# Moving the residual adds of a down projection, the end of an attention chunk and the last norm's scaling

## The chip, the cores and the metric

The kernel runs on one core of a Trainium2 chip. The metric is the device time of one execution in microseconds (us). The kernel before takes 2182.29 us, the median of three runs (2181.57 to 2185.2). The engines are named as in the profile: PE (TensorE) with its weight loads PEld, DVE (VectorE), ACT (ScalarE), POOL (GpSimd), and SP (SyncE), whose queue issues all DMAs of this kernel.

## The reference

One decoder layer on x of 2048 positions by 1024 columns, in float32. A norm and one input projection feed two mixers: chunked gated linear attention with 4 heads (GLA), and a short convolution. An output projection and the residual follow, then a SwiGLU feed-forward network with its residual, then a last norm:

```
h = rmsnorm(x, norm1_g);  proj = h @ w_in
o_gla = rmsnorm(gla_chunked(q, k, v, log_a), gla_norm_g) * silu(p_g)
x = x + concat([o_gla, o_conv]) @ w_out
h2 = rmsnorm(x, norm2_g)
x = x + (silu(h2 @ w_ffn_gate) * (h2 @ w_ffn_up)) @ w_ffn_down
return rmsnorm(x, norm_f_g)          # D_MODEL 1024, D_FF 2816
```

## The kernel before, in words

The positions are worked on in two halves of 1024, each as two blocks j of 512 columns; the 1024 features are 8 tiles of 128 rows (d = 0 to 7, `KD`). A tile is 128 partitions by 512 float32, 256 KB. Every float32 matrix product is made of three passes on high and low parts: `split` turns a tile into a rounded high part (ACT, L144) and the remainder (DVE, L145), and `product_step` (L316) issues high·high, high·low and low·high (L321, L322, L323).

The large projections are cut into **units**. A `unit` (L325) computes a 2 by 2 block of result tiles (two row tiles r, two column blocks j) in Strassen's manner: seven products in place of eight, in the order of `PRODUCTS` (L34). Its weights come in one load (`raw`, two buffers); `unit_weights` (L298) makes four sums of weight quarters on POOL (L304, L305, L306, L311) and splits seven quarters into `wq` tiles (four buffers). Its operands ("B11", "T1", ...) were stored as high and low pairs of 512 KB (`op`, pool `opp`, 28 buffers). Results collect in PSUM banks; `copied` (L341, ACT) takes a bank to an SBUF tile, `plus` (L345, DVE) adds a bank to one.

The stages run in this order: input projection of half 0 and half 1 (GLA's work of a half beside it), output projection of both halves, and then for each half `ffn_up` and `ffn_down`. Smaller work is written as generators in the list `background`; `tick` (in `mul`) advances the first of them by one step after every second product. `split_later` and `store_split` write the feed-forward operands through three buffers `so` to the DRAM tensors shown as sa_B and sa_T. `bt` takes a tile from a pool of 11 buffers in this part of the kernel (`fx`).

`gla_half` (L569) is such a generator. For every chunk of 128 positions it makes the scores, yields, loads the next chunk and makes the outputs (`gla_outputs`, L628, which ends with `osb`, L662), yields, and finishes the chunk (`gla_finish`, L665: four transposes of `osb` into the bank `ot`, L669; the product with gain and gate, L670; a split; stores), and yields.

`ffn_down` (L836) runs over four groups u of hidden row pairs (two, three, three and three), and within each over four units (d0 = 0, 2, 4, 6), 16 units per half. The result tiles y[d, j] gather all groups. In u = 0 the sixteen tiles y are first loaded from the residual s_x1 (shown as sx; L846 to L851), seven pairs in buffers of `opp`. Each unit's four results are then added to y, three by POOL and the one still in PSUM by DVE (L862 to L865). In the last group, half 0 stores y for `finish_later`, which norms it in the background of half 1; half 1 sums squares on the way (`sum_squares`, L691) and ends with `last_unit` (L892), which computes eight half products without the seven-product scheme, makes rstd per block (`norm`, L901, `finish_rstd`, L163), and scales by gain and rstd in `scale` (L907): five tiles per block by DVE in one three-operand operation (L914), three by ACT and POOL (L911, L912).

The order on each engine is set by a scheduler in the build, which models the instructions' times and waits; within SP's queue the DMAs go out one after the other, and one that waits holds those behind it. `tc.issue_after` keeps an instruction behind another in that order.

Of the kernel before, what the change touches and what calls it, by code (L numbers as in the profile page):

```python
# [10 lines left out]
F32 = mybir.dt.float32  # L11
# [36 lines left out]
def tile_hymba_block(ctx, tc, x, xt, win, wa, wgu, wout, wffn, wdown, wdown_first, small, out):  # L48
# [30 lines left out]
    )  # L79
    one_t = ones[:, 0:1]  # L80
    sml = const.tile([P, N_SMALL], F32, name="sml")
    nc.sync.dma_start(sml[:], small)
# [64 lines left out]
    def rsqrt(y, v, l, y0):  # L147

        act.activation(l, v, AF.Ln)
        act.activation(y0, l, AF.Exp, scale=-0.5)  # L150
        dve.tensor_tensor(l, y0, y0, ALU.mult)
        dve.scalar_tensor_tensor(l, l, -0.5, v, ALU.mult, ALU.mult)
        dve.scalar_tensor_tensor(y, l, 1.5, y0, ALU.add, ALU.mult)
# [8 lines left out]

    def finish_rstd(v, tot, n):  # L163
        l, y0 = bt("l"), bt("y0")
        dve.tensor_scalar(v[:], tot[:], 1.0 / n, EPS, ALU.mult, ALU.add)
        rsqrt(v[:], v[:], l[:], y0[:])

# [156 lines left out]

    def unit(src, ops):  # L325


        w = unit_weights(src)

        def mul(i, o=None):  # L330
            first = o is None
            o = bank() if first else o
            n, m = PRODUCTS[i]
            for k in range(len(ops[m])):
                product_step(o, w[n], ops[m], k, first)
            tick()
            return o

        def copied(name, o):
            t = tt(name)  # L340
            act.activation(t[:], o[:], AF.Copy)  # L341
            return t

        def plus(t, o):
            dve.tensor_tensor(t[:], o[:], t[:], ALU.add)  # L345
            return t


        oa = mul(0)
        c11 = copied("c11", oa)  # L350
        ob = mul(1)
        c22 = copied("c22", ob)
        mul(2, oa)
        c12 = copied("c12", oa)
        plus(c11, mul(3))
        mul(4, oa)
        plus(c22, oa)
        mul(5, ob)
        plus(c12, ob)
        mul(6, oa)  # L360
        return [(0, 0, c11, False), (1, 1, c22, False), (0, 1, c12, False), (1, 0, oa, True)]

# [206 lines left out]
    def gla_half(half):  # L569
# [3 lines left out]
        with tc.issue_after(tables.ins):  # L573
            nxt = gla_load(*chunks[0])
        for n, (b, t) in enumerate(chunks):
            cur = nxt
            s = gla_scores(b, t, *cur)
            yield
            if n + 1 < len(chunks):
                nxt = gla_load(*chunks[n + 1])  # L580
            o = gla_outputs(b, t, *s)
            yield
            gla_finish(b, t, *o)
            done.add((b, t))
            yield

# [249 lines left out]
    def ffn_down(half):  # L836

        y = {}
        for u, m0 in enumerate(GROUPS):
# [52 lines left out]
    def last_unit(src, ops, b12, y, ssq):  # L892
# [7 lines left out]

        def norm(j, qs):  # L901
            tot = bank("tot")
            for i, q in enumerate(qs):
                pe.matmul(tot[:], ones[:], q[:], start=i == 0, stop=i == len(qs) - 1)
            finish_rstd(qs[0], tot, D)

        def scale(j, rb):  # L907
            for d in range(KD):
                yy = y[d, j]
                if d % 3 == 1:  # L910
                    act.activation(yy, yy, AF.Copy, scale=col(C_GF + d))  # L911
                    pool.tensor_tensor(yy, yy, rb[:], ALU.mult)  # L912
                else:
                    dve.scalar_tensor_tensor(  # L914
                        yy, yy, col(C_GF + d), rb[:], ALU.mult, ALU.mult
                    )
                load(out[2 + j, :, d, :], yy)

        qs = [ssq[:1], ssq[1:]]
        for j in range(2):  # L920
            for r in range(2):
# [8 lines left out]
                dve.tensor_tensor(yy, o[:], yy, ALU.add)  # L930
                q = tt("q")
                act.activation(q[:], yy, AF.Square)
                qs[j].append(q)
                if j and not r:
                    norm(0, qs[0])
        norm(1, qs[1])
        for j in range(2):
            scale(j, qs[j][0])

# [132 lines left out]
```

## Time and profile before

| what | value |
|---|---|
| median of three runs | 2182.29 us |
| profiled execution | 2184.78 us |
| its span, first to last instruction | 2183.0 us |
| granted PE clock, mean | 0.982 |
| DMA: moved, mean rate | 467.65 MB, 214 GB/s |
| first product of u = 0 on PE, half 0 and half 1 | 1264.49 and 1915.31 us |
| end of VectorE's last operation | 2177.78 us |

All times inside the kernel are from the span's start. A row of the timeline is start, length, engine, line, operation, tiles and count, and in brackets the idle time before it with what ended it. A row of the waits is the engine and line that waited, what ended the wait, the total, the count and the longest. A row of the groups is busy time and mean ns of one, then the idle time of the engine before them and what ended it. In a row of the windows, each engine's busy time has its instruction count behind it, and the last three numbers are the granted clock, the DMA engines' mean busy share and GB/s. A line such as `op<-sa_T` is an operand load, `raw<-in_wdown_first_dram` the weights of a unit of u = 0.

### The profile page before, as it was taken

Reading aid. Unit: us, or ns where it says so; the run is one execution under the profiler, and the core shown is the slowest. Engines: PE = TensorE matmul, PEld = TensorE weight load, DVE = VectorE, ACT = ScalarE, POOL = GpSimd, SP = SyncE. Lnnn points to the kernel's source line nnn. Section 1 sums busy time; section 2 is a strip of 40 time slices with the busy share of each in tenths; the row PEclk is TensorE's granted clock in tenths of the full one; section 3 lists DMA queues with packets and bytes.
Section 4 is the critical chain, followed back from the end, with each engine's and each line's share of the span. In section 5 each row is a group of like instructions: output and inputs, shape, how many; then the busy total and the mean of one; then the engine's idle time right before and its main releaser. Section 6 shows DMA issues by size and latency. Waiting matters only on the chain.

```text
span 2183.0 us, 26899 instructions
## 1 busy us (share of the span) xinstructions
PE 2048.8 (94%) x9137; PEld 1656.3 (76%) x9137; DVE 1460.2 (67%) x2039; ACT 996.5 (46%) x1940; POOL 985.5 (45%) x706
## 2 busy tenths in 40 slices
PE   4899899999998999999999989998999999989996
PEld 3577677877887887788888868887888888867774
DVE  7859975557763496787877566544666656668755
ACT  4555434564544245455555433333444544434442
POOL 4526431112201273555655456664544445357663
PEclk9999999999999999999999999999999999999998
DMA  4259667532586793466454595698353443598772
GB/s 147 71 202 321 215 246 258 150 111 91 156 289 198 295 309 138 164 234 223 174 227 174 214 357 209 245 347 348 116 183 135 159 160 134 221 361 315 304 266 101
DMA packets 189978, 467.65 MB, mean 214 GB/s; under 512 B 19856, under 2 KB 65168, under 8 KB 180112
## 3 DMA queue, kind: packets, MB, share of 16 engines
q1 hardware_dynamic: 189840, 465.93, 59.2%
q8 instruction: 72, 1.18, 0.2%
q14 instruction: 66, 0.54, 0.1%
HBM read 297.03 MB, written 168.82 MB: 213 GB/s over the span
## 4 chain that ended last, share of the span: by engine, by line
PE 68%; DVE 13%; DMA 9%; ACT 4%; issue 3%; POOL 2%; SPq 1%; DVEq 0%; ACTq 0%; POOLq 0%
PE mm L321 20%; PE mm L323 20%; PE mm L322 20%; DVE wq L145 2%; DVE h L431 2%; DMA op<-shT 1%; DVE op L145 1%; PE mm L709 1%; PE mm L710 1%; PE mm L712 1%; DMA op<-sm 1%; DMA op<-sa_T 1%; DVE c L345 1%; DMA raw<-in_wdown_first_dram 1%; DVE so L145 1%
## 5 line engine op out<-in xcount | busy, mean ns | idle before, releaser
L321 PE MATMUL mm<-op,wq 128*128 128x512 f32 x2495 | 984.2, 396 | 50.9 <-ACT c L341 22.2
L322 PE MATMUL mm<-op,wq 128*128 128x512 f32 x2495 | 977.9, 392 | 4.1 <-DVE op L145 4.1
L323 PE MATMUL mm<-op,wq 128*128 128x512 f32 x2495 | 967.2, 393 | 14.9 <-DVE wq L145 14.5
L145 DVE TENSOR_TENSOR wq<-raw,wq 128x512 fp32r<-128x512 f32 (+2 forms) x628 | 526.6, 845 | 337.8 <-ACT wq L144 335.6
L144 ACT ACTIVATE wq<-raw 128x512 fp32r<-128x512 f32 (+2 forms) x628 | 365.1, 587 | 580.2 <-PE mm L323 408.3
L321 PEld LDWEIGHTS mm<-op,wq 128*128 128x128 f32 x2495 | 471.7, 189 | 167.7 <-ACT c L341 30.7
L323 PEld LDWEIGHTS mm<-op,wq 128*128 128x128 f32 x2495 | 471.6, 189 | 124.7 <-DVE wq L145 24.4
L322 PEld LDWEIGHTS mm<-op,wq 128*128 128x128 f32 x2495 | 472.1, 189 | 102.9 <-DVE op L145 5.1
L306 POOL TENSOR_TENSOR raw<-s,raw 128x512 f32<-128x512 f32 (+2 forms) x98 | 131.5, 1342 | 461.5 <-DVE wq L145 427.2
L345 DVE TENSOR_TENSOR c<-mm,c 128x512 f32<-128x512 f32 x294 | 201.6, 686 | 102.6 <-PE mm L323 97.9
L304 POOL TENSOR_TENSOR s<-raw 128x512 f32<-128x512 f32 (+2 forms) x98 | 130.9, 1336 | 210.8 <-DMA raw<-in_wffn_dram 90.5
L341 ACT ACTIVATE c<-mm 128x512 f32<-128x512 f32 x294 | 170.7, 586 | 31.9 <-PE mm L323 30.8
L311 POOL TENSOR_TENSOR raw<-raw 128x512 f32<-128x512 f32 (+2 forms) x98 | 129.0, 1317 | 119.7 <-DVE wq L145 104.2
L865 POOL TENSOR_TENSOR y<-c,y 128x512 f32<-128x512 f32 x90 | 135.9, 1515 | 92.0 <-DVE c L345 91.8
L691 POOL TENSOR_TENSOR ssx<-ssx,q 128x512 f32<-128x512 f32 x52 | 75.9, 1472 | 144.1 <-ACT q L690 143.6
L305 POOL TENSOR_TENSOR raw<-raw 128x512 f32<-128x512 f32 (+2 forms) x98 | 137.2, 1400 | 4.7
L145 DVE TENSOR_TENSOR so<-t,so 128x512 fp32r<-128x512 f32 x100 | 88.0, 889 | 40.2 <-ACT so L144 39.9
L709 PE MATMUL mm<-op,wq 128*128 128x512 f32 x256 | 101.3, 396 | 0.0
L710 PE MATMUL mm<-op,wq 128*128 128x512 f32 x256 | 100.5, 393 | 0.0
L144 ACT ACTIVATE wq<-s 128x512 fp32r<-128x512 f32 (+2 forms) x98 | 57.5, 587 | 92.0 <-PE mm L323 87.6
L144 ACT ACTIVATE so<-t 128x512 fp32r<-128x512 f32 x100 | 62.7, 629 | 66.5 <-DMA sa_B<-so 35.3
L145 DVE TENSOR_TENSOR wq<-s,wq 128x512 fp32r<-128x512 f32 (+2 forms) x98 | 79.3, 810 | 14.8 <-ACT wq L144 14.2
(170 smaller groups left out, 1856.2 us busy)
## 6 DMA issues: line engine op xcount, KB each, us to landing
raw<-in_wffn_dram SPq DMA_DIRECT2D x44, 1024.0 KB, 5.6
sa_T<-so SPq DMA_DIRECT2D x88, 512.0 KB, 5.0
op<-sa_T SPq DMA_DIRECT2D x88, 512.0 KB, 8.4
sa_B<-so SPq DMA_DIRECT2D x69, 512.0 KB, 3.8
op<-sa_B SPq DMA_DIRECT2D x69, 512.0 KB, 8.6
raw<-in_win_dram SPq DMA_DIRECT2D x24, 1024.0 KB, 5.9
raw<-in_wdown_dram SPq DMA_DIRECT2D x24, 768.0 KB, 6.8
y<-sx SPq DMA_DIRECT2D x64, 256.0 KB, 6.7
```

What stands on the lines that cost most here:

```text
L144: last_hi[:] = [act.activation(hi, src, AF.Copy)]
L145: return dve.tensor_tensor(lo, src, hi.bitcast(F32), ALU.subtract)
L304: pool.tensor_tensor(s1, a21, a22, ALU.add)
L305: pool.tensor_tensor(a21, a11, a21, ALU.subtract)
L306: pool.tensor_tensor(a11, s1, a11, ALU.subtract)
L311: pool.tensor_tensor(a12, a12, a11, ALU.subtract)
L321: pe.matmul(o[:], wh, xh, start=first and k == 0, stop=False, skip_group_check=True)
L322: pe.matmul(o[:], wh, xl, start=False, stop=False, skip_group_check=True)
L323: return pe.matmul(o[:], wl, xh, start=False, stop=k == n - 1, skip_group_check=True)
L341: act.activation(t[:], o[:], AF.Copy)
L345: dve.tensor_tensor(t[:], o[:], t[:], ALU.add)
L865: eng.tensor_tensor(yy, c[:], yy, ALU.add)
```

## The change

- **finish_rstd.** ACT's Ln reads the summed squares straight from PSUM, with scale and bias in the same instruction; VectorE still makes the scaled sum for the Newton step, which is now a function of its own and can write into a PSUM bank.
- **unit(into=...).** In u = 0 the unit copies and adds its results directly in the tiles y, which aren't loaded with residuals; the fourth result is also copied by ACT. In u = 1 and u = 2 each unit loads two residual tiles (`x1`, for j = u - 1) and POOL adds them to y after the unit's own adds.
- **gla_half.** A chunk's finish comes after the next chunk's scores; the last one's comes at the end.
- **last_unit.** The gains are applied by ACT ahead of the norm (all sixteen tiles), the squares of r = 0 are added by POOL to the running sum so that the norm sums two tiles instead of three, and rstd stays in PSUM (`rb`), from which VectorE scales six tiles per block; ACT copies it to SBUF for POOL's two tiles.

```diff
+    eps = const.tile([P, 1], F32, name="eps")
+    dve.memset(eps[:], EPS)
...
         act.activation(y0, l, AF.Exp, scale=-0.5)
+        newton(y, v, l, y0)
+
+    def newton(y, v, l, y0):
         dve.tensor_tensor(l, y0, y0, ALU.mult)
...
-    def finish_rstd(v, tot, n):
+    def finish_rstd(v, tot, n, rb=None):
         l, y0 = bt("l"), bt("y0")
+        act.activation(l[:], tot[:], AF.Ln, bias=eps[:], scale=1.0 / n)
+        act.activation(y0[:], l[:], AF.Exp, scale=-0.5)
         dve.tensor_scalar(v[:], tot[:], 1.0 / n, EPS, ALU.mult, ALU.add)
-        rsqrt(v[:], v[:], l[:], y0[:])
+        newton((v if rb is None else rb)[:], v[:], l[:], y0[:])
...
-    def unit(src, ops):
+    def unit(src, ops, into=None):
...
-        def copied(name, o):
-            t = tt(name)
+        def copied(name, o, at):
+            t = tt(name) if into is None else into[at]
...
         mul(6, oa)
+        if into is not None:
+            copied("c21", oa, (1, 0))
...
+        o = None
         for n, (b, t) in enumerate(chunks):
             cur = nxt
             s = gla_scores(b, t, *cur)
             yield
+            if o is not None:
+                gla_finish(*chunks[n - 1], *o)
+                yield
             if n + 1 < len(chunks):
                 nxt = gla_load(*chunks[n + 1])
             o = gla_outputs(b, t, *s)
             yield
-            gla_finish(b, t, *o)
-            done.add((b, t))
-            yield
+        gla_finish(b, t, *o)
+        done.add((b, t))
+        yield
...
-            if u == 0:
-                for d in range(KD):
-                    pair = opp.tile([P, 2, PB], F32, name="y", tag="op") if d < KD - 1 else None
-                    for j in range(2):
-                        y[d, j] = bt("y")[:] if pair is None else pair[:, j, :]
-                        with tc.issue_after(raw_loads[-1].ins):
-                            load(y[d, j], s_x1[2 * half + j][d][:])
...
+                if u == 0:
+                    for d in (d0, d0 + 1):
+                        if d < KD - 1:
+                            pair = opp.tile([P, 2, PB], F32, name="y", tag="op")
+                        for j in range(2):
+                            y[d, j] = pair[:, j, :] if d < KD - 1 else bt("y")[:]
+                    unit(src, ops, {(r, j): y[d0 + r, j] for r in range(2) for j in range(2)})
+                    continue
+                xs = []
+                if u < 3:
+                    for d in (d0, d0 + 1):
+                        xs.append((y[d, u - 1], bt("x1")))
+                        load(xs[-1][1][:], s_x1[2 * half + u - 1][d][:])
...
+                for yy, x1 in xs:
+                    pool.tensor_tensor(yy, x1[:], yy, ALU.add)
...
-        def norm(j, qs):
-            tot = bank("tot")
-            for i, q in enumerate(qs):
-                pe.matmul(tot[:], ones[:], q[:], start=i == 0, stop=i == len(qs) - 1)
-            finish_rstd(qs[0], tot, D)
+        def gain(d, j):
+            act.activation(y[d, j], y[d, j], AF.Copy, scale=col(C_GF + d))
+
+        def norm(j, q):
+
+            tot, rb = bank("tot"), bank("rb")
+            pe.matmul(tot[:], ones[:], ssq[j][:], start=True, stop=False)
+            pe.matmul(tot[:], ones[:], q[:], start=False, stop=True)
+            finish_rstd(ssq[j], tot, D, rb)
+            act.activation(ssq[j][:], rb[:], AF.Copy)
+            return rb
 
         def scale(j, rb):
             for d in range(KD):
-                yy = y[d, j]
-                if d % 3 == 1:
-                    act.activation(yy, yy, AF.Copy, scale=col(C_GF + d))
-                    pool.tensor_tensor(yy, yy, rb[:], ALU.mult)
-                else:
-                    dve.scalar_tensor_tensor(
-                        yy, yy, col(C_GF + d), rb[:], ALU.mult, ALU.mult
-                    )
-                load(out[2 + j, :, d, :], yy)
+                eng, by = (pool, ssq[j]) if d in (2, 5) else (dve, rb)
+                eng.tensor_tensor(y[d, j], y[d, j], by[:], ALU.mult)
+                store(out[2 + j, :, d, :], y[d, j])
+
+        for d in range(KD - 2):
+            for j in range(2):
+                gain(d, j)
...
-                q = tt("q")
-                act.activation(q[:], yy, AF.Square)
-                qs[j].append(q)
+                q[j] = tt("q")
+                act.activation(q[j][:], yy, AF.Square)
+                gain(KD - 2 + r, j)
+                if not r:
+                    pool.tensor_tensor(ssq[j][:], ssq[j][:], q[j][:], ALU.add)
                 if j and not r:
-                    norm(0, qs[0])
-        norm(1, qs[1])
+                    rbs.append(norm(0, q[0]))
+        rbs.append(norm(1, q[1]))
```

More of the change, by code (lines that the diff above doesn't have):

```diff
@@ L349, in unit @@
         oa = mul(0)
-        c11 = copied("c11", oa)
+        c11 = copied("c11", oa, (0, 0))
         ob = mul(1)
-        c22 = copied("c22", ob)
+        c22 = copied("c22", ob, (1, 1))
         mul(2, oa)
-        c12 = copied("c12", oa)
+        c12 = copied("c12", oa, (0, 1))
         plus(c11, mul(3))
@@ L899, in last_unit @@
             act.preload_act_table_set("natural_log_exp_and_others")
-        def norm(j, qs):
-            tot = bank("tot")
-            for i, q in enumerate(qs):
-                pe.matmul(tot[:], ones[:], q[:], start=i == 0, stop=i == len(qs) - 1)
-            finish_rstd(qs[0], tot, D)
+        def gain(d, j):
[7 more added lines that the diff above has]
+            return rb
         def scale(j, rb):
             for d in range(KD):
-                yy = y[d, j]
-                if d % 3 == 1:
-                    act.activation(yy, yy, AF.Copy, scale=col(C_GF + d))
-                    pool.tensor_tensor(yy, yy, rb[:], ALU.mult)
-                else:
-                    dve.scalar_tensor_tensor(
-                        yy, yy, col(C_GF + d), rb[:], ALU.mult, ALU.mult
-                    )
-                load(out[2 + j, :, d, :], yy)
-        qs = [ssq[:1], ssq[1:]]
+                eng, by = (pool, ssq[j]) if d in (2, 5) else (dve, rb)
[4 more added lines that the diff above has]
+                gain(d, j)
+        q, rbs = {}, []
         for j in range(2):
@@ L930, in last_unit @@
                 dve.tensor_tensor(yy, o[:], yy, ALU.add)
-                q = tt("q")
-                act.activation(q[:], yy, AF.Square)
-                qs[j].append(q)
+                q[j] = tt("q")
[3 more added lines that the diff above has]
+                    pool.tensor_tensor(ssq[j][:], ssq[j][:], q[j][:], ALU.add)
                 if j and not r:
-                    norm(0, qs[0])
-        norm(1, qs[1])
+                    rbs.append(norm(0, q[0]))
+        rbs.append(norm(1, q[1]))
         for j in range(2):
-            scale(j, qs[j][0])
+            scale(j, rbs[j])
     act.preload_act_table_set("natural_log_exp_and_others")
```

## The prediction

> **What bounds the kernel now.** I read the page first: the engines' busy times, then the chain that ended last.
>
> ```profile
> span 2183.0 us, 26899 instructions
> PE 2048.8 (94%) x9137; PEld 1656.3 (76%) x9137; DVE 1460.2 (67%) x2039; ACT 996.5 (46%) x1940; POOL 985.5 (45%) x706
> PE 68%; DVE 13%; DMA 9%; ACT 4%; issue 3%; POOL 2%; SPq 1%; DVEq 0%; ACTq 0%; POOLq 0%
> ```
>
> TensorE (PE) is busy for 94% of the span and the chain runs mostly through its matmuls. The change leaves these as they are, but for two norm matmuls less. So a gain can only come out of the span less PE's busy time, 2183.0 - 2048.8 = 134 us, and out of stretches with a slow clock. I therefore looked for the places where PE stops beside the changed code. Next come windows: the first two group units of each half's down projection up to the start of group u1 (half 0, then half 1), two slices inside the first stall, the slice after it, and a stretch without a stall. The columns are the length, the busy time of PE, PEld, DVE, ACT and POOL with their instructions, the granted clock, DMA's share and GB/s.
>
> ```profile
> 1264.49:1316.07 51.58, 42.34 (x176) 33.78 (x174) 34.78 (x51) 20.42 (x46) 32.20 (x30) 0.90 0.89 343
> 1915.31:1970.35 55.04, 44.24 (x178) 34.06 (x177) 40.31 (x53) 23.75 (x52) 34.90 (x31) 0.91 0.94 359
> 1290.00:1295.00 5.00, 0.00 (x0) 0.00 (x0) 0.69 (x1) 1.21 (x2) 0.00 (x0) 0.54 1.03 419
> 1295.00:1300.00 5.00, 3.77 (x9) 3.00 (x10) 3.21 (x5) 2.67 (x8) 3.85 (x5) 0.50 0.81 329
> 2005.00:2037.00 32.00, 32.00 (x140) 25.75 (x138) 22.49 (x26) 16.05 (x34) 30.32 (x24) 1.00 0.77 293
> ```
>
> The last row gives PE's pace: 32.00/140 = 0.229 us a matmul. At that pace the first two rows need 176 x 0.229 = 40.3 and 178 x 0.229 = 40.8 us. They take 51.58 and 55.04, so **11.3 and 14.3 us are lost in group u0**. In the middle of the loss PE does nothing while DMA is full (share 1.03, 419 GB/s), and after it the granted clock is 0.50 for some 5 us. The waits of the two places say who comes last (half 0, then half 1):
>
> ```profile
> ACT so L144 <- DMA sa_B<-so: 10.3, 2, 9.9
> PE mm L321 <- ACT wq L144: 8.5, 1, 8.5
> POOL s L304 <- DMA raw<-in_wdown_first_dram: 7.8, 1, 7.8
> ```
>
> ```profile
> ACT so L144 <- DMA sa_B<-so: 11.3, 2, 10.6
> PE mm L321 <- ACT wq L144: 9.3, 1, 9.3
> POOL s L304 <- DMA raw<-in_wdown_first_dram: 8.7, 1, 8.7
> ```
>
> PE waits for ACT's weight split, ACT is held in its queue by a split for a store buffer (so) whose store hasn't gone out, and unit 2's weights (raw) land late too. Both are DMAs that stand in SyncE's queue behind the residual loads, as SP's timeline shows:
>
> ```profile
> 1261.38 14.04 SPq L136 DMA_DIRECT2D y<-sx  x14
> 1275.81 0.32 SPq L139 DMA_DIRECT2D sa_B<-so  x1
> 1276.48 1.67 SPq L136 DMA_DIRECT2D op<-sa_B  x3
> 1278.52 2.40 SPq L136 DMA_DIRECT2D op<-sa_T  x4
> 1281.70 1.59 SPq L136 DMA_DIRECT2D y<-sx  x2
> 1284.41 1.48 SPq L139 DMA_DIRECT2D sa_B<-so  x2
> 1286.86 1.61 SPq L136 DMA_DIRECT2D raw<-in_wdown_first_dram  x2
> ```
>
> **The change part by part.** The sum is made against the profiled execution: 2184.78 us, 1.78 more than its span and 2.49 above the median of 2182.29; its differences are then taken off the median.
>
> *Group u0.* The sixteen 256 KB loads of y go, and the stores and the third raw load no longer stand behind them. They took SP from 1261.38 to about 1275.4. In the built order the third raw load then has only stores and no op load ahead of it, so I expect it at about 1275 instead of 1286.86, and the so buffers come free as much earlier. Unit 2 then starts without a stop and the clock stays up. The whole loss is the most this can give: 11.3 + 14.3 = 25.6 us.
>
> What is late next? SP is in order, and in the built program the weight load for u1's first unit now stands ahead of all 21 operand loads of u1, of which seven (three and four in the rows above) went out before. That load waits for its buffer, that is for the last split of unit 2. Unit 2 would start at about 1287 and last some ten us, so the buffer comes free at about 1292. DMA's own rate over this stretch is this row, from the DMA view of 1242 to 1297:
>
> ```profile
> DMA packets 7132, 21.78 MB, mean 396 GB/s; under 512 B 796, under 2 KB 796, under 8 KB 7129
> ```
>
> 512 KB (0.524 MB) at 396 GB/s is 1.32 us; 21 of them are 27.8 us, and the weights ahead of them (0.79 MB) 2 us. The last operand lands at about 1292 + 2 + 27.8 = 1322, or 1324 with two us to land. u1 would start 11.3 us earlier, at 1304.8, and its first unit (63 matmuls, 14.4 us) ask for that operand near 1318 to 1319. **New wait: 4 us in half 0**, and 5 in half 1, where two 256 KB x1 loads share the queue with it. At best it is 0, at worst it takes all back. I take u0 at -(11.3 - 4) - (14.3 - 5) = **-16.6 us**, bounds -25.6 and 0. The adds that go (twelve on Pool, four on VectorE per half) were off the path; the four copies that come, 0.6 us each like L149, are hidden by ACT having 20.42 us of work in 51.58, and would cost 2.4 us per half without that cover.
>
> The Trainium skill, "TensorE: Matmul & The Clock Gate", section "HAM oscillation — how this bites in real kernels", holds that an idle gap above about 3.4 us drops TensorE to half rate; the 0.50 row agrees. By that rule a residual wait in one piece would cost up to its own drop again, about 2 us per half, and in pieces nothing. I keep the pieces.
>
> *Groups u1 and u2.* Each of 16 units gets two 256 KB loads and two adds on Pool. The adds that u0 loses stood elsewhere, so here the work is more. Pool's cover is read by group (half 0 u1 and u2, half 1 u1 and u2; four units of 14.3 us each); then come the group of Pool's adds and, for later, a VectorE add with one operand in PSUM:
>
> ```profile
> 1316.00:1373.00 57.00, 57.00 (x254) 47.18 (x253) 33.76 (x46) 20.67 (x41) 37.45 (x30) 1.00 0.60 226
> 1373.00:1430.00 57.00, 57.00 (x252) 46.92 (x251) 28.54 (x44) 20.10 (x40) 35.55 (x29) 1.00 0.64 246
> 1971.00:2028.00 57.00, 56.77 (x248) 45.87 (x248) 47.04 (x57) 25.47 (x51) 45.49 (x34) 1.00 0.85 317
> 2028.00:2085.00 57.00, 52.73 (x226) 41.77 (x225) 41.35 (x52) 21.58 (x40) 38.31 (x29) 1.00 0.75 281
> ```
>
> ```profile
> L865 POOL TENSOR_TENSOR y<-c,y 128x512 f32<-128x512 f32 x90 | 135.9, 1515 | 92.0 <-DVE c L345 91.8
> ```
>
> ```profile
> L734 DVE TENSOR_TENSOR y<-y,mm x32: 669/678/690, 660.4 to 833.8; 128x512 f32<-128x512 f32 x32
> ```
>
> An add takes 1.515 us, eight of them 12.1 us per group. Pool then has 49.6, 47.7, 57.6 and 50.4 us of work in 57. Three groups keep 6 us or more free. In u1 of half 1 Pool is full, 0.6 us over. Queued behind an x1 add are the next unit's weight sums (L304 to L311), for which ACT's splits wait, and then PE. I take **+3 us**: the 0.6 and about 2.4 where sums come late; bounds 0 and 12.1, the whole of u1's adds.
>
> Here a rule speaks against the change. The Trainium skill, "SBUF — State Buffer", section "Who interferes with whom", says that a VectorE instruction with two SBUF inputs and a GpSimd instruction that reads SBUF lock each other out for a whole instruction. By it every added Pool add can hold up one weight split for up to 1.5 us, 12 us on top of VectorE's 47.04 in u1 of half 1. That is 59 of 57, and the sum would be about +2 more. It bears on the rival below.
>
> *Attention chunks.* The transposes of a chunk's output (ot, L669) are what PE waits on:
>
> ```profile
> L669 PE MATMUL ot<-ident,osb 128*128 128x128 f32 x64 | 10.2, 284 | 11.2 <-DVE osb L662 11.2
> ```
>
> ```profile
> 658.86 5.57 DMA y<-in_xt_dram
> 664.56 0.69 DVE y L734
> 665.99 1.08 PE ot L669 x4
> ```
>
> The second fence is cut from the chain at the largest case: VectorE's L662, which makes osb, comes behind an L734 that waits for a DMA, and the transposes behind both. With the chunk's end a step later, 12 to 56 matmuls (2.7 to 12.8 us at 0.229) stand between in the built order; the three waits together are 11.2 us. I take **-10.5 us**: 0.7 stays. If PE merely waits for the next thing of that same late VectorE queue, -0 to -4 is left; so bounds -11.2 and 0.
>
> *The last norm.* Before, VectorE and SP end the program in this order:
>
> ```profile
> 2159.29 0.68 DVE L930 TENSOR_TENSOR y<-mm,y 128x512 f32<-128x512 f32 x1
> 2160.61 6.53 DVE L914 SCALAR_TENSOR_TENSOR y<-y,sml,ssx 128x512 f32<-128x512 f32 x5
> 2167.06 0.68 DVE L165 TENSOR_SCALAR ssx<-tot 128x512 f32<-128x512 f32 x1
> 2171.27 6.51 DVE L914 SCALAR_TENSOR_TENSOR y<-y,sml,ssx 128x512 f32<-128x512 f32 x5
> ```
>
> ```profile
> 2162.51 16.40 SPq L136 DMA_DIRECT2D out_dram<-y  x16
> ```
>
> ```profile
> L912 POOL TENSOR_TENSOR y<-y,ssx 128x512 f32<-128x512 f32 x6 | 9.2, 1562 | 18.3 <-DVE ssx L153 18.3
> L914 DVE SCALAR_TENSOR_TENSOR y<-y,sml,ssx 128x512 f32<-128x512 f32 x10 | 13.0, 1366 | 0.1
> L149 ACT ACTIVATE l<-ssx 128x512 f32<-128x512 f32 x6 | 3.8, 632 | 9.8 <-DVE ssx L165 9.8
> ```
>
> The last scale ends at 2171.27 + 6.51 = 2177.78. After: the six products of j=0 read rstd in PSUM, and a two-operand VectorE op with one operand there took 0.68 (L734) against 1.3 for L914: 6 x 0.68 = 4.1 us, from 2159.9 to 2164.0. In the built order the last L930 stands behind them, to 2164.7. Then come ACT's square 0.63, the second norm's matmuls (estimated at four paces, 0.9), Ln and Exp 2 x 0.63, three VectorE steps 2.1 (0.68 to 0.7 each, as L165) and six products 4.1: 2164.7 + 9.0 = 2173.7. Pool's two products, 0.63 + 2 x 1.56 from 2169.6, end at 2173.3. So -4.1 (the stores behind it as before), and +0.5 for sixteen gains on ACT in u3: **-3.6 us**, bounds -5.5 and +2 (all six at L914's 1.3).
>
> *finish_rstd.* VectorE's step beside Exp instead of ahead of Ln saves 0.68 at most where PE waits for a norm, at the start: **-0.5**, bounds -0.7 and 0.
>
> Sum: -16.6 + 3 - 10.5 - 3.6 - 0.5 = **-28.2 us**; 2184.78 becomes 2156.6, and the median 2182.29 becomes **2154.1**.
>
> **The rivals.** *A, DMA keeps up:* u1's operands come in time because the queue drains during units 2 and 3, and Pool has room. For it: DMA's share is only 0.60 in u1 of half 0. Against it: 419 GB/s at full share while 21 loads are due. u0 -25.6, Pool 0: -40.2, 2142.1. *B, the wait moves on:* PE leaves ot and stands at the next matmul that needs a split from the same blocked VectorE. For it: the L734 ahead waits for DMA either way. Against it: weights are split up to four quarters ahead. -28.2 + 8 = -20.2, 2162.1. *C, Pool half bound:* the sums come late in u1 and u2 of half 1, 12 us instead of 3: -19.2, 2163; with B, 2171. *D, slower:* Pool is the bound in u1 and u2. Its queue is in order, so every x1 add stands ahead of the next unit's weight sums and delays them; SP too stands at an x1 load whose buffer that add must free, with the next weights behind it. 32 adds x 1.515 = 48.5 us instead of 3 gives -28.2 + 45.5 = +17.3, 2199.6. It decides for slower once more than 28.2 + 3 = 31.2 us, 21 of the 32 adds, are on the path. For it: 45.49 of 57. Against it: 6 us or more free in the three other groups. *E:* the change doesn't do what it says; the built order shows the y loads gone from u0 and the chunk ends later, so hardly.
>
> **How the numbers follow.** Forecast (2147 to 2159) 0.47; A 0.15; B or C or both (2159 to 2173) 0.25; D and parts of it 0.09; within 0.2% of before, with E, 0.04. 0.2% (4.4 us) is about what a measurement of this kernel can tell from no change. Faster 0.87, same 0.04, slower 0.09. The range holds the forecast, A with a little more at its low end, and B and C: 2138 to 2173; D lies outside.
>
> **What would show it.** In the changed kernel's profile: the windows at u0 have no slice with PE at 0 and clock 0.5; the third raw load goes out near 1275 less what the chunks gave; new PE waits of a few us at the start of u1 end in op<-sa_T or op<-sa_B DMAs; L669 has under 1 us of idle; the scales stand at 0.69 and the last ends about 4 us nearer to PE's last product. Wrong would be: PE waits for ACT wq with Pool L306 or L311 behind it for over 10 us in u1 and u2 (D), a 9 us stop at u0 still there, or an idle time of some 8 us that turns up at other lines of the attention stretch (B).

## The result and the profile after

The changed kernel takes **2169.37 us** (median of five runs, 2163.8 to 2172.21) against 2182.29 us before (five runs, 2177.67 to 2187.82). The medians differ by 12.9 us. The ratio is 0.9933, with a 95% interval of 0.9916 to 0.9951: 0.67% or some 14.6 us faster (10.7 to 18.3), about half of the 28.2 us that were forecast. The profiled execution took 2172.21 us and is the slowest of the five; keep that in mind where two traces are compared by absolute times. Differences of stages suffer less from it: a second kernel with the same down projection (the second of experiment 1) repeats the rows below within 1.8 us.

The page after, its engines and its chain:

```profile
span 2170.2 us, 26909 instructions
PE 2055.1 (95%) x9133; PEld 1658.8 (76%) x9133; DVE 1447.5 (67%) x2034; ACT 1009.1 (46%) x1960; POOL 993.6 (46%) x714
PE 71%; DVE 11%; DMA 8%; issue 4%; ACT 3%; POOL 3%; SPq 1%; DVEq 0%; POOLq 0%; ACTq 0%
```

The line numbers are now the changed kernel's: a split is L146 (ACT) and L147 (VectorE), a unit's three passes L328 to L330, its weight sums L311 to L318, the adds to y L884 and the added x1 adds L891.

PE's idle time fell from 134 to 115 us, but its modelled busy time rose by 6, since matmuls that trickle in are counted longer (in u1's first unit below, 19.84 us for 74 after against 16.30 before). To find the stages, I cut both traces at the same matmuls. The three passes of the units come in the same order and number in both (2495 each), so the n-th of them in one is the n-th in the other. That gives windows with equal work, with edges within a few matmuls of the groups': u0 of half 0, u1's first unit (72 matmuls, nine of them the next unit's), the same two in half 1, and there the **last stretch**, from that point to the end of u2's first unit. Before:

```profile
1265.80:1316.10 50.30, 41.06 (x170) 32.69 (x170) 33.70 (x49) 20.00 (x45) 31.75 (x29) 0.90 0.89 341
1316.10:1332.40 16.30, 16.30 (x74) 13.49 (x73) 10.31 (x14) 6.25 (x13) 10.94 (x9) 1.00 0.99 398
1913.90:1971.70 57.80, 47.00 (x189) 36.25 (x189) 42.15 (x56) 25.08 (x54) 36.61 (x32) 0.91 0.94 362
1971.70:1988.50 16.80, 16.67 (x73) 13.44 (x73) 15.60 (x19) 7.64 (x15) 11.55 (x9) 1.00 1.03 402
1988.50:2047.20 58.70, 56.97 (x246) 45.43 (x245) 44.43 (x54) 26.74 (x51) 46.32 (x35) 1.00 0.85 322
```

After:

```profile
1252.30:1291.00 38.70, 38.58 (x169) 31.40 (x168) 29.61 (x46) 22.17 (x48) 18.45 (x19) 1.00 0.67 262
1291.00:1315.00 24.00, 19.84 (x74) 13.24 (x73) 7.53 (x12) 5.83 (x12) 8.59 (x8) 0.97 1.03 406
1899.80:1945.70 45.90, 43.74 (x189) 35.02 (x188) 35.04 (x55) 28.29 (x57) 21.42 (x21) 1.00 0.81 317
1945.70:1969.60 23.90, 20.54 (x74) 14.02 (x74) 10.37 (x17) 7.04 (x14) 9.70 (x9) 0.93 1.03 405
1969.60:2036.90 67.30, 59.78 (x245) 46.42 (x244) 46.93 (x53) 26.70 (x51) 54.92 (x41) 0.95 0.91 341
```

Read the rows pairwise, by length. Group u0 went from 50.30 to 38.70 and from 57.80 to 45.90: **23.5 us gained**, with PE idle for 0.1 and 2.2 us instead of 9.2 and 10.8 and the clock at 1.00. Right behind it u1's first unit went from 16.30 to 24.00 and from 16.80 to 23.90: **14.8 us given back**, with DMA full (1.03). In half 1 the last stretch went from 58.70 to 67.30: **8.6 us more given back**, with Pool at 54.92 us instead of 46.32. Of these 8.6 us, 5.8 are idle time of PE (7.5 instead of 1.7) and 2.8 slower matmuls at a clock of 0.95 instead of 1.00. These stages alone sum to 0. The gain that is left lies elsewhere: 12.8 us from the first unit's first product to u0 of half 0, where the attention chunks are, and 4.1 behind the last product (20.3 us instead of 24.4). Against it stand 3.3 us between the rows of the two halves and 1.6 between the last stretch and the last product.

The operand waits are seen in the waits of the changed kernel from 1291 to 1315, the cause in SP's timeline ahead of it:

```profile
ACT wq L146 <- DMA raw<-in_wdown_dram: 11.4, 1, 11.4
...
PEld mm L328 <- DMA op<-sa_B: 2.9, 4, 0.8
```

```profile
1269.90 0.37 SPq L138 DMA_DIRECT2D raw<-in_wdown_first_dram  x1
1279.01 0.33 SPq L138 DMA_DIRECT2D raw<-in_wdown_dram  x1
1279.43 1.64 SPq L138 DMA_DIRECT2D op<-sa_B  x3
1281.16 3.77 SPq L138 DMA_DIRECT2D op<-sa_T  x6
1287.44 2.88 SPq L138 DMA_DIRECT2D op<-sa_B  x3
1291.28 2.88 SPq L138 DMA_DIRECT2D op<-sa_T  x3
1295.12 2.88 SPq L138 DMA_DIRECT2D op<-sa_B  x3
```

SP issues nothing between 1270.3 and 1279.0: it stands at u1's weights, whose buffer isn't free, and all 21 operand loads are behind. The waits for op come in pieces of at most 0.8 us. ACT's wait of 11.4 us is for the next weights, those of u1's second unit: they go out at 1300.25 behind most of the operands, ACT splits them at 1311.12, and PE stops for 1.5 us.

The attention chunks' transposes, L669 before, wait for nothing now:

```profile
L682 PE MATMUL ot<-ident,osb 128*128 128x128 f32 x64 | 9.6, 273 | 0.0
```

The end, four of VectorE's rows from the last unit on:

```profile
2150.68 3.68 DVE L937 TENSOR_TENSOR y<-y,rb 128x512 f32<-128x512 f32 x6 [0.66 <-ACT ssx L931]
2154.27 0.69 DVE L954 TENSOR_TENSOR y<-mm,y 128x512 f32<-128x512 f32 x1
2157.68 0.69 DVE L172 TENSOR_SCALAR ssx<-tot 128x512 f32<-128x512 f32 x1 [2.73 <-ACT l L170]
2161.16 3.68 DVE L937 TENSOR_TENSOR y<-y,rb 128x512 f32<-128x512 f32 x6 [0.66 <-ACT ssx L931]
```

Six scales take 3.68 us instead of 6.5 for five, and the last residual add (L954) stands behind the first six, as the order of the program had it. The last scale ends at 2164.84.

### The profile page after: what moved, and what is told of

Same layout as the page of the kernel before. It is cut to its first block, busy times and chain, and to the rows that moved or that the text cites. A ratio compares the mean times of both kernels' runs of the same rounds, so it can differ in the third digit from the quotient of the medians.

```text
span 2170.2 us, 26909 instructions
## 1 busy us (share of the span) xinstructions
PE 2055.1 (95%) x9133; PEld 1658.8 (76%) x9133; DVE 1447.5 (67%) x2034; ACT 1009.1 (46%) x1960; POOL 993.6 (46%) x714
## 4 chain that ended last, share of the span: by engine, by line
PE 71%; DVE 11%; DMA 8%; issue 4%; ACT 3%; POOL 3%; SPq 1%; DVEq 0%; POOLq 0%; ACTq 0%
PE mm L328 21%; PE mm L330 21%; PE mm L329 20%; DVE wq L147 2%; DVE h L440 2%; DMA op<-sa_T 2%; PE mm L722 2%; PE mm L725 2%; PE mm L723 2%; DMA raw<-in_wdown_dram 1%; DVE op L147 1%; DMA op<-sa_B 1%; DVE so L147 1%; ACT wq L146 1%; DVE c L352 1%
## 5 line engine op out<-in xcount | busy, mean ns | idle before, releaser
L328 PE MATMUL mm<-op,wq 128*128 128x512 f32 x2495 | 987.7, 398 | 38.6 <-ACT c L348 18.2
L330 PE MATMUL mm<-op,wq 128*128 128x512 f32 x2495 | 972.0, 394 | 18.8 <-DVE wq L147 18.0
L147 DVE TENSOR_TENSOR wq<-raw,wq 128x512 fp32r<-128x512 f32 (+2 forms) x628 | 532.1, 854 | 345.0 <-ACT wq L146 338.9
L146 ACT ACTIVATE wq<-raw 128x512 fp32r<-128x512 f32 (+2 forms) x628 | 365.2, 587 | 583.4 <-PE mm L330 408.5
L328 PEld LDWEIGHTS mm<-op,wq 128*128 128x128 f32 x2495 | 473.4, 190 | 159.1 <-ACT c L348 25.4
L330 PEld LDWEIGHTS mm<-op,wq 128*128 128x128 f32 x2495 | 473.4, 190 | 130.4 <-DVE wq L147 30.7
L352 DVE TENSOR_TENSOR c<-mm,c 128x512 f32<-128x512 f32 x270 | 185.2, 686 | 101.2 <-PE mm L330 98.5
L311 POOL TENSOR_TENSOR s<-raw 128x512 f32<-128x512 f32 (+2 forms) x98 | 131.0, 1337 | 197.7 <-DMA raw<-in_wffn_dram 87.5
L318 POOL TENSOR_TENSOR raw<-raw 128x512 f32<-128x512 f32 (+2 forms) x98 | 129.9, 1326 | 128.9 <-DVE wq L147 119.8
L348 ACT ACTIVATE c<-mm 128x512 f32<-128x512 f32 x270 | 156.7, 585 | 31.3 <-PE mm L330 30.2
L884 POOL TENSOR_TENSOR y<-c,y 128x512 f32<-128x512 f32 x66 | 98.9, 1500 | 72.4 <-DVE c L352 68.9
L147 DVE TENSOR_TENSOR so<-t,so 128x512 fp32r<-128x512 f32 x100 | 87.9, 885 | 26.0 <-ACT so L146 25.8
L146 ACT ACTIVATE wq<-s 128x512 fp32r<-128x512 f32 (+2 forms) x98 | 57.5, 587 | 94.5 <-PE mm L330 91.8
L147 DVE TENSOR_TENSOR wq<-s,wq 128x512 fp32r<-128x512 f32 (+2 forms) x98 | 77.6, 792 | 17.0 <-ACT wq L146 16.4
L146 ACT ACTIVATE so<-t 128x512 fp32r<-128x512 f32 x100 | 62.8, 629 | 42.8 <-DMA sa_T<-so 17.6
```

Of the source, the lines that this page charges most:

```text
L146: last_hi[:] = [act.activation(hi, src, AF.Copy)]
L147: return dve.tensor_tensor(lo, src, hi.bitcast(F32), ALU.subtract)
L311: pool.tensor_tensor(s1, a21, a22, ALU.add)
L328: pe.matmul(o[:], wh, xh, start=first and k == 0, stop=False, skip_group_check=True)
L330: return pe.matmul(o[:], wl, xh, start=False, stop=k == n - 1, skip_group_check=True)
```

## The experiments

Eleven kernels were run. Each was compared with the kernel before on its own chip; the medians of before were 2184.4 to 2184.9 there, so ratios are the better measure.

**1. The three parts, each alone on the kernel before.** The edits are the three parts of the diff above: `gla_half`; `unit(into=...)` with `ffn_down`; and `finish_rstd` with `last_unit`.

> The kernel before with the later chunk ends alone. Theory (the transposes' waits are gone and nothing takes their place): 10 to 13 us below before, most of it at the largest wait near 660 us. Rival B of the prediction (the wait moves to the next matmul that needs the same VectorE queue): 2 to 7 us below. If the gain of the changed kernel ahead of the feed-forward stage came from the norm's new form instead: under 2 us.

Measured: 2166.79 us, ratio 0.992 (0.990 to 0.994), 17.5 us below before (13 to 22 by the interval). This is more than the theory asked. Its transposes wait for nothing, as after. Two rows, 640 to 680 us, show where a good part comes from (this kernel, then before):

```profile
640.00:680.00 40.00, 40.00 (x222) 32.98 (x221) 17.06 (x41) 17.76 (x49) 2.56 (x2) 1.00 0.81 260
```

```profile
640.00:680.00 40.00, 33.33 (x185) 27.28 (x184) 13.72 (x30) 13.50 (x35) 2.85 (x2) 0.91 0.90 292
```

The stop there cost not only its 6.7 us of idle time. The clock of 0.91 is the mean of the whole row, and half of its low stretch lies in the stop itself; behind the stop, from 666 to 671 us, it was 0.69, which is 1.6 us more. Against it, one stop of PE of 3.7 us is new, at the scores of a chunk near 347 us. It is not shown to be rival B: the profile names nothing that ended it, and by 380 us this trace is as far ahead as it was before the stop. The rest of the gain lies in smaller steps, 2.1 near 466 and some 4 between 830 and 910, whose cause I didn't trace.

> The kernel before with the down projection's part alone (results straight into y in u0, x1 added in u1 and u2). Theory from the two traces: the stops in u0 go (about 24 us), and the operand waits in u1 and the later Pool-bound places give 26 to 30 us back, so 2 to 6 us above before. Rival, the prediction's own sum: new operand wait 9 and Pool 3, so 13.6 us below before. Third: if the 7 us loss near 2020 to 2031 of the changed kernel comes from the new norm and not from this part, 1 to 5 us below before.

Measured: 2187.67 us, ratio 1.0009 (0.9997 to 1.0022), 2 us above before, not separable from no change. The theory read from the traces fits, and the prediction's sum for this part (13.6 below) falls. Its stage rows are those of the changed kernel: 38.6 and 45.3 for u0, 24.3 and 24.0 for u1's first unit, and

```profile
1974.80:2043.90 69.10, 60.95 (x246) 46.92 (x245) 48.24 (x54) 26.74 (x52) 54.88 (x41) 0.93 0.88 336
```

for the last stretch, so the third reading, that the norm's new form makes that loss, falls as well.

> The kernel before with the norm's new form and the last unit's new scaling alone. Theory: about 4 us below before at the very end (six scales of 0.69 instead of five of 1.3, and the last norm not behind them) and under 1 at the start: 4 to 5 below. Rival: Ln waiting in ACT's queue for the summed squares delays weight splits behind it in half 1's background norms; then the gain shrinks to 0 to 2 us.

Measured: 2181.68 us, ratio 0.999 (0.9979 to 1.0001), 2.2 us below before: between the two, and not separable from no change. The trace gives both: the end after the last product shrank from 24.4 to 20.7 us, and in half 1's background norms, from 2037 to 2047, 2 to 3 us were lost. The three parts alone sum to -17.5 + 2.0 - 2.2 = -17.7 us, near the 14.6 measured together.

**2. The operand loads of u1 ahead of its weights.** In the changed kernel, the seventh operand load is what u1's first weights are issued after, and the eighth is issued after these.

```diff
+        if u_now[0] == 1 and len(op_loads) == 7:
+            with tc.issue_after(op_loads[-1].ins):
+                early.append(raw_weights(wdown[0]))
...
-        raw = raw_weights(src)
+        raw = early.pop() if early else raw_weights(src)
```

> The changed kernel with one thing moved: seven of u1's 21 operand loads go out ahead of the weights of u1's first unit, as they did before, in both halves. Theory (that weight load, waiting for its buffer, holds the operand loads in SP's queue): the loads start some 9 us earlier, the waits for op in u1 shrink from 7 us to under 2 in each half, and the time is 9 to 14 us below the changed kernel, if nothing else is late at once. Rival (the DMA rate alone makes the operands late, 21 loads of 1.3 us): the loads start earlier but the last lands no more than 2 us earlier, and the time is within 3 us of the changed kernel.

Measured: 2170.8 us, ratio 0.9937 (0.9915 to 0.9958): no faster than the changed kernel. The time is the rival's, the mechanism the theory's: SP now issues seven operands from 1267.7 on and the last of the 21 near 1293 instead of 1303, PE waits for no op in either unit, and u1's first unit takes 18.0 us instead of 24 in both halves. But in half 1 two other stages took it back. First, u0, then u1's first unit and the last stretch:

```profile
1890.60:1941.70 51.10, 45.41 (x189) 35.39 (x188) 35.11 (x56) 28.53 (x58) 21.16 (x20) 0.96 0.89 342
1941.70:1959.70 18.00, 18.00 (x72) 14.53 (x72) 8.78 (x13) 5.40 (x12) 8.15 (x7) 0.91 1.04 406
1959.70:2032.00 72.30, 62.28 (x245) 47.23 (x245) 49.70 (x55) 27.87 (x54) 58.32 (x44) 0.93 0.83 311
```

u0 has 51.10 instead of 45.90, and the last stretch 72.30 instead of 67.30. In u0 PE stops for 2.65 us at a matmul that waits for VectorE's L352, which stands there between the steps of a background norm, then for 1.1 us for a weight split, and runs on at half the clock. Why the order is this one I didn't isolate. In the last stretch Pool has 58.32 us of work.

**3. Pool's adds.** First the changed kernel with each x1 add cut to one column; the loads and buffers stay. The kernel leaves out most of the residual, so its result isn't that of the reference.

```diff
-                    pool.tensor_tensor(yy, x1[:], yy, ALU.add)
+                    pool.tensor_tensor(x1[:, 0:1], x1[:, 0:1], yy[:, 0:1], ALU.add)
```

> The changed kernel with the 32 x1 adds on Pool cut to one column each; the x1 loads and their buffers stay (the residual is left out of the result). Theory (Pool's added work is what delays the weight sums in u1 and u2): the loss near 2020 to 2031 (7 us) goes with most of the 1.3 us steps in u1 and u2, and the time is 7 to 12 us below the changed kernel. Rival (the loads in SP's queue, not the adds, make the losses): within 3 us of the changed kernel.

Measured: 2154.81 us, ratio 0.9866 (0.9848 to 0.9885). By the ratios this is 14.6 us below the changed kernel, somewhat more than was expected. The rows of u1's first unit (half 0 and 1) and of the last stretch:

```profile
1285.60:1309.90 24.30, 20.23 (x73) 13.58 (x72) 7.70 (x13) 6.03 (x12) 8.37 (x8) 0.95 1.03 406
1937.30:1960.90 23.60, 20.22 (x73) 13.73 (x72) 9.75 (x16) 6.80 (x14) 8.54 (x9) 0.93 1.03 405
1960.90:2022.60 61.70, 58.22 (x245) 46.71 (x244) 43.79 (x54) 27.51 (x52) 46.59 (x41) 0.97 0.95 357
```

The two causes come apart: u1's first unit is as slow as with the adds (24.30 and 23.60), for its operands are late all the same, and the last stretch fell from 67.30 to 61.70. From there to the last product another 4.5 us went (113.0 to 108.5). So the adds cost about 10 us in half 1. How they cost it is not settled by this run, for two things go with them: Pool's queue gets shorter, and VectorE's weight splits (L147 on raw, 128x384) take 884 ns on the mean in the last stretch instead of 1114. What stays there, 61.70 against 58.70 before, is as much as the norm's part alone loses (61.6 in its run); yet with the old norms the adds lose no less (69.10 above), so the two don't simply add. The two profiled executions differ by 18.4 us; 5.4 of these lie ahead of the down projection, where the two kernels do the same, and show the spread of single executions.

Then the adds on VectorE, together with the order of experiment 2 (its edit, and `dve` for `pool` in the line above).

> The kernel with seven operand loads ahead of u1's weights, and the x1 adds on VectorE instead of Pool. Theory (the operand loads gave back on Pool in half 1 what they won): 9 to 18 us below the changed kernel, with no loss near 2020 to 2031 and under 2 us of op waits in each u1. Rival (VectorE, at 40 of 57 us in u1 of half 1, is late with its splits instead): within 4 us of the changed kernel.

Measured: 2165.65 us, ratio 0.9915 (0.9896 to 0.9933), 3.9 below the changed kernel by the ratios, which their intervals don't separate: the rival's size. The last stretch:

```profile
1962.80:2031.60 68.80, 62.08 (x245) 47.63 (x245) 56.87 (x63) 27.96 (x54) 49.23 (x36) 0.93 0.89 329
```

Pool is down to 49.23, but VectorE is up to 56.87 from 46.93, and the stretch is 3.5 us shorter than in experiment 2 but no shorter than in the changed kernel (67.30). The rival's reason is not shown: PE waits for VectorE's splits for 2.3 us there, against 2.7 in the changed kernel. In half 1 neither Pool nor VectorE takes the sixteen adds for nothing.

**4. Without the down projection's part.** The kernel before with the other two parts.

> The change without its down projection part: later chunk ends and the norms only. If the parts add up as measured alone, 17.5 + 2.2 us: 19 to 20 us below before, that is 4 to 6 below the changed kernel. If the parts overlap (the norm's gain at the end is lost in half 1's background norms): 15 to 17 us below before.

Measured: 2166.5 us, ratio 0.9917 (0.9896 to 0.9939), 18.1 us below before: between the two sums, and ahead of the changed kernel by 3 us, which their intervals don't separate.

**5. Only the place of the y loads.** That kernel, with the sixteen loads of y no longer asked for together ahead of u0's units; each unit asks for its own four. The adds stay where they were.

```diff
-            if u == 0:
-                for d in range(KD):
...
+                results = unit(src, ops)
+                if u == 0:
+                    for d in (d0, d0 + 1):
...
+                            with tc.issue_after(raw_loads[-1].ins):
+                                load(y[d, j], s_x1[2 * half + j][d][:])
```

> The run before with the y loads of u0 asked for unit by unit instead of all sixteen ahead; the residual adds stay as they were before, on Pool and VectorE, in no other group. Theory (only the place of the y loads in SP's queue made the stops of 9 us, and the x1 adds give the gain back): the stops shrink to under 3 us in each half, no Pool loss in half 1, and the time is 12 to 22 us below the run without the down projection's part. Rival (DMA is full there, and the loads only move the wait to the operands of u1, 7 us in each half): 0 to 8 us below it.

Measured: **2158.27 us**, ratio 0.9877 (0.9857 to 0.9897), the fastest of all that compute the whole: 26.6 us below before, 8.2 below the run without the down part (its slowest execution took 2159.82, the other's fastest 2164.38). Its stages, u0 and u1's first unit in half 0 and then half 1, and the last stretch:

```profile
1245.60:1287.90 42.30, 39.81 (x169) 30.61 (x167) 34.54 (x48) 19.24 (x44) 31.03 (x27) 1.00 0.99 378
1287.90:1306.60 18.70, 17.35 (x73) 13.39 (x73) 8.30 (x12) 6.17 (x13) 12.15 (x11) 1.00 1.00 401
1887.00:1935.50 48.50, 45.40 (x189) 34.22 (x187) 41.01 (x55) 25.89 (x55) 37.88 (x32) 1.00 1.01 392
1935.50:1956.70 21.20, 18.76 (x73) 14.53 (x73) 10.99 (x17) 6.24 (x13) 9.09 (x8) 0.92 1.03 407
1956.70:2019.70 63.00, 57.26 (x246) 45.31 (x245) 48.51 (x57) 27.84 (x53) 48.12 (x36) 1.00 0.84 316
```

The long stop is gone without a single add moved (42.30 and 48.50 against 50.30 and 57.80 before; clock 1.00). Some comes back in u1's first unit (18.70 and 21.20). The total lies between the theory (12 to 22) and the rival (0 to 8), at the rival's edge.

**6. The norm's form.** `column_rstd` goes back to VectorE's step ahead of Ln; the last unit keeps the new form.

```diff
-        finish_rstd(rb, tot, n)
+        l, y0 = bt("l"), bt("y0")
+        dve.tensor_scalar(rb[:], tot[:], 1.0 / n, EPS, ALU.mult, ALU.add)
+        rsqrt(rb[:], rb[:], l[:], y0[:])
```

On the run of experiment 5, and on the changed kernel:

> The run with y loaded unit by unit, with the norm's old form (VectorE ahead of Ln) everywhere but in the last unit. Theory (in half 1's background norms the new form stands 4 us longer in front of the weight splits on ACT and VectorE): 2 to 5 us below that run, so some 1.4% below before. Rival (those splits wait for Pool's sums anyway): within 1.5 us of it.

> The changed kernel with the norm's old form everywhere but in the last unit. Theory (the 7 us loss near 2020 to 2031 is Pool's, with at most 3 of the norm): 0 to 3 us below the changed kernel, the loss there still 4 us or more. Rival (the loss is the norm's): 5 to 8 us below it, and the loss there under 2 us.

Measured: 2162.49 us, ratio 0.991 (0.9892 to 0.9928), so above the run of experiment 5 and not below, by 4 us of the medians and 7 of the ratios, whose intervals just touch: both readings miss. If anything the new form helps there, by 2.2 us in the last stretch (65.2 against 63.0). On the changed kernel 2168.34 us, ratio 0.993 (0.9915 to 0.9945), 0.7 below by the ratios: the loss in the last stretch stays (69.2), so it isn't the norm's, as the theory had it.

**7. Experiment 5 without the norm's part** (later chunk ends and y by unit alone).

> The kernel before with the later chunk ends and with y loaded unit by unit; norms and last unit as before. Theory (the norm's part wins 4 us at the end and gives 4 back in u1 and u2 of half 1, so it is worth nothing beside the others): within 2.5 us of the run that has all three (2158.3 us), with the stage from u1's second unit to the end of u2 in half 1 at 59 to 61 us instead of 63.0. Rival (that stage is as slow without the norm's part, from the operands that now come later): 3 to 5 us above that run.

Measured: 2166.18 us, ratio 0.9926 (0.9903 to 0.9949), 7.9 above the run with all three by the medians and 10.7 by the ratios: the theory falls, and it is more than the rival's 3 to 5. The last stretch is 65.2 us, as in experiment 6. At the last product this trace is 9.2 us behind that of the run with all three, but 4.9 of these lie ahead of the down projection, where the run with the later chunk ends alone, with the same code up to there, was 3.5 us shorter: part of it is the spread of single executions. Alone, the norm's part gains 2.2 us, within the noise; beside the y loads by unit it is worth more. Why its new form costs 3 to 4 us in the last stretch when little else is early and gains 2 when u0 is shorter is not settled; the order of the weight splits on ACT differs in each of these programs, and I didn't isolate it.

## Why the prediction was right, and where its sum failed

The direction and the range (2138 to 2173) held; the time came out at 2169.4 instead of 2154.1. That is above the forecast's own 2147 to 2159, in the part that was left to rivals B and C. That it is still in the range is partly luck, for two errors of the sum cancel: the down projection was put at -13.6 and gave +2.0 alone, and the attention chunks were put at -10.5 and gave -17.5 alone. Point by point:

- **Group u0.** "The whole loss is the most this can give", 25.6 us, held: 23.5 measured. The third raw load went out at 1261.42 (1275 less the 13.5 us that this kernel is ahead there), with no slice at half clock.
- **The new wait** ("4 us in half 0, and 5 in half 1") had the right mechanism, the weight load that stands in SP's queue ahead of 21 operand loads, and for the operands nearly the right size. In half 0 the first 38 of the unit's 63 matmuls go at full pace, and the others follow the loads, one operand every 1.28 us. From its first matmul to its last the unit takes 18.8 and 20.2 us instead of 14.1, so 4.8 and 6.2 more. 21 loads at 1.32 us are 27.7 us of DMA for a unit that computes for 14.4, so late operands can't be made up within it. What the sum lacks is what follows, up to the 14.8 us of both halves: in half 0 the second unit's weights come late (1.7 us), and in both halves the clock falls to 0.50 for over 3 us (1313.5 to 1316.8, 1965.5 to 1968.7), 1.2 and 0.7 us more. "In pieces nothing" did not hold: no stop of PE there was longer than 1.5 us.
- **Pool in u1 and u2** ("+3, bounds 0 and 12.1") failed most. The last stretch alone cost 8.6 us in the changed kernel, and without the adds the time falls by about 10 us in half 1. The prediction saw that Pool is full in u1 of half 1 (57.6 of 57), and took the surplus of 0.6 and 2.4 us for late sums. PE's waits in the last stretch, before and after:

```profile
PE mm L321 <- ACT wq L144: 1.6, 1, 1.6
```

```profile
PE mm L328 <- ACT wq L146: 3.9, 2, 3.4
PE mm L330 <- DVE wq L147: 2.7, 3, 1.6
```

  The longest of them, 3.4 us at 2027.9, is followed back in these rows of Pool and then ACT:

```profile
2016.30 1.63 POOL L891 TENSOR_TENSOR y<-x,y 128x512 f32<-128x512 f32 x1
2017.89 1.61 POOL L704 TENSOR_TENSOR ssx<-ssx,q 128x512 f32<-128x512 f32 x1
2019.46 1.59 POOL L884 TENSOR_TENSOR y<-c,y 128x512 f32<-128x512 f32 x1
2021.00 1.01 POOL L318 TENSOR_TENSOR raw<-raw 128x384 f32<-128x384 f32 x1
```

```profile
2022.05 0.94 ACT L146 ACTIVATE wq<-raw 128x384 fp32r<-128x384 f32 x2 [4.59 <-POOL raw L318]
2027.32 0.51 ACT L146 ACTIVATE wq<-raw 128x384 fp32r<-128x384 f32 x1
```

  Pool works without a pause there. The weight sum L318 comes behind an x1 add (L891) and two other adds, ACT's splits wait 4.59 us for it, and the split that PE waits for (2027.32) stands behind Ln, Exp and two table loads of a background norm as well (2023.49 to 2027.4). So an add in a nearly full in-order queue can make the sums behind it late by its whole length, whether or not the mean has room. That this is most of the loss is argued from this one place: the prediction's other price, weight splits of VectorE held up by Pool's adds (12 us in the group), shows too, as 230 ns on each of 24 splits (5.5 us; experiment 3), and no run separates the two. The group of added adds after is 47.1 us of work:

```profile
L891 POOL TENSOR_TENSOR y<-x,y 128x512 f32<-128x512 f32 x32 | 47.1, 1473 | 6.7 <-DVE y L884 6.1
```

  About a fifth of it reached PE's path in half 1, and by the medians of the whole at most a third (14.6 us), far from rival D's all. Rival C (12 instead of 3) was the nearest.
- **Attention chunks** ("-10.5") was too small: alone the part gives 17.5 us. In the traces, the three kernels without it need 1206.5 to 1209.1 us from the first unit's first product to u0 of half 0 and the ten with it 1189.1 to 1196.3, so it is worth about 15. Of what the sum lacks, 1.6 us are the half-rate clock behind the largest stop, left out here though the same effect was counted in u0; some 4 lie between 830 and 910 us, and their cause stays open.
- **The last norm** ("-3.6") held where it stands: from the last product's start to the last scale, 2177.78 - 2158.62 = 19.2 us became 2164.84 - 2149.89 = 15.0, so -4.2. Alone it gave only 2.2 in all, which isn't separable from nothing; the reason is left open above.
- **finish_rstd** at the start ("-0.5"): the first product of the units comes 0.7 us earlier, at 56.07 instead of 56.80. That shows nothing, for with the down projection's part alone, whose norms are the old ones, it came at 55.48.

The down projection's part is thus the odd one out: it won 23.5 us at u0 and lost them within two groups. That "Three groups keep 6 us or more free" did not help: in the fourth alone 8.6 us went.

The Trainium skill, "SBUF — State Buffer", section "Who interferes with whom", states that a VectorE instruction with at most one SBUF input, outside the two-port modes, doesn't contend with GpSimd. The tail agrees: VectorE's six scales with rstd in PSUM take 0.61 us each, five of them beside Pool's two products. Before, with both operands in SBUF, the mean was 1.3, and it is a mean of two kinds:

```profile
L914 DVE SCALAR_TENSOR_TENSOR y<-y,sml,ssx x10: 737/1744/1869, 2160.6 to 2177.1; 128x512 f32<-128x512 f32 x10
```

The six beside a product of Pool took 1.74 to 1.87 us, and the four behind Pool's last one 0.74. So most of the gain of the new form is that it keeps clear of Pool. Pool's own products fell from 1.56 to 1.27 us at the same time (9.2 us for six before, 5.0 for four after).

## What to carry to other kernels

When loads stand in an in-order queue ahead of something urgent, first ask for them later or in parts (8.2 us here, experiment 5); moving the work that needs them to other stages moves load onto engines that may be full there. Compute the idle room of the engine that gets the work in the very stage, and take a nearly full in-order queue as exposed, not as covered by its mean. And cut two traces at the same matmuls: a gain that is given back within 100 us is invisible in the total, and plain in the stage rows.

## What the runs showed of the hardware that was not expected

A stop of PE costs about a quarter more than its length by the clock. Behind the stop of 6.7 us at 666 us in the kernel before, the clock was 0.69 over 5 us (1.6 us more); behind the stops of 8.5 and 9.3 us in u0 it was 0.50 for 4.4 and 4.6 us (2.2 and 2.3 more). Many short waits can do the same: in u1's first unit of the changed kernel the clock fell to 0.50 for over 3 us in both halves, though PE never stood still for more than 1.5 us at once.

At the end, VectorE's scales waited for ACT's copy of the same rstd bank (0.66 us, both times in the rows of the end), though both only read it. Whether the build asks for that order or the chip, and what another order would give, wasn't tried.
